# A two-layer decoder trunk: RMSNorm factors sent through DRAM instead of TensorE, and their sums over four column groups

## The chip, the cores and the metric

The kernel runs on one core of a Trainium2 chip. The metric is the device time of one execution, in microseconds (us). A core has five engines that run side by side, each through its own list of instructions in order: TensorE (PE in the profile, with its weight loads as PEld), VectorE (DVE), ScalarE (ACT), GpSimd (POOL) and SyncE (SP). All matrix products end in PSUM, a small memory in eight banks; everything else lives in SBUF, a memory of 128 partitions, or in DRAM, which DMA transfers reach.

## The reference

Two layers; in each, one RMSNorm feeds two token mixers, and their gated sum goes through an output projection into the residual stream. There are 512 tokens and 16 learned meta tokens ahead of them (T = 528), a width of 1024 and fp32 data.

```python
h = rmsnorm(h_res, norm_gain[l])                  # over 1024 channels
proj = h @ w_in[l]
u_pool, z_pool, c_q, c_kv, k_rope, z_mla, g_pool, g_mla = jnp.split(proj, IN_SPLIT_POINTS, axis=-1)
y_pool = (pool_mix(u_pool, pool_w_group[l], pool_scale[l]) * jax.nn.silu(z_pool)) @ pool_w_up[l]
o_mla = mla(c_q, c_kv, k_rope, pos, ...)          # 8 heads; c_kv is normed over 256 channels
y_mla = (o_mla * jax.nn.silu(z_mla)) @ mla_w_up[l]
merged = jax.nn.sigmoid(g_pool) * y_pool + jax.nn.sigmoid(g_mla) * y_mla
h_res = h_res + merged @ w_out[l]
```

`pool_mix` takes, for four groups of 128 channels, the mean over the last 2, 4, 8 or 16 tokens minus the token itself, and multiplies by a 128 x 128 matrix. A norm's factor is 1/sqrt(mean of squares + eps), one number per token; two of them matter here, that of h and that of c_kv.

## The kernel before

**Layout.** Channels lie on partitions and tokens along the free dimension, so a tile is 128 channels x 528 tokens. A projection (class `Gemm`) makes one such tile: for each 128 rows of its weights, three matmuls (`mm3`, L190 to L192) on high and low halves of weights and data, which together give nearly fp32 precision. The first layer and the whole-sequence tiles of the second go in two segments of 264 tokens (`FULL`); other tiles of the second layer go in one of 512 (`XS`).

**Factors after the product.** The product is taken on data that isn't normed, and the factor of each token is applied when a tile is evicted from PSUM. So u (L491), the gates (L500, L563, L882) and k_rope (L446) multiply by `inv`, and the k tiles by `cinv` (L574). Both are tiles of 128 equal rows x 528 tokens: a row has to be spread over all partitions.

**How the factors are made** (`norm_sums`). The squares of the eight x tiles (`xsq`) and of the two c_kv tiles (`csq`) are summed over partitions by matmuls with a matrix of ones, 32 columns wide (L363). `tile_position=(0, g)` puts such a matmul on the column group g (0, 32, 64 or 96) of the array. Before, the x sums of the two segments are in groups 0 and 64, and the c sums in 32 and 96. The sums are copied to SBUF (L370), five small transposes (L375, L376) turn them into one number per partition, and VectorE runs three Newton steps for the inverse root on a 128 x 10 tile (`newton`, L294 to L300). For the way back, `rows` transposes the result to rows (L404 to L407), ScalarE copies it to `kinv` (L409, L410), and `spread` multiplies it by a selection matrix, so that each row appears on all 128 partitions (L286), and copies that to SBUF (L287). A similar return exists in the kernel for the keys' factors: eight rows go to DRAM (`kdr`, L692) and come back as broadcasts (`bc`, L701).

**The order of the work.** A generator (`stream`) walks through the projections in the order in which `register` lists them and adds up planned TensorE time: n/2.4 ns for a matmul of n columns. `Layer.go` runs beside it. `up(name)` takes the stream to the end of a projection, `fill_now(ns)` takes it on by so much planned time, and what `go` issues in between stands at that place in program order. Weights come in chunks of 128 x 512, loaded from SP's queue (L114; three buffers) and split into halves by ScalarE (L185) and VectorE (L186); kr's weights are multiplied by the norm gain instead (L181). The framework's planner then lays out each engine's list: program order is the priority, and an instruction whose inputs, by the planner's own times, aren't ready yet is passed by later ones. So the Newton steps on VectorE have splits and evictions between them.

**The stretch in question.** ckv0, ckv1, cq0 to cq2, u0, k0, u1, kr, k1, u2, k2, u3, k3, cq3, v, the four zp with y0 to y2, cq4, y3, cq5. `norm_sums` starts behind ckv1. The first that needs `inv` is the eviction of u0, the first that needs `cinv` that of k0. `tables` (sine and cosine for the rotary part, L304 to L314, layer 0 alone) comes behind u0. `mix(m)` builds the windowed mean of group m by m+1 additions on GpSimd (L513) and two to four VectorE operations (L516 to L520), and splits it for y(m).

Of the kernel before, what the change touches and what calls it, by code (L numbers as in the profile page):

```python
# [18 lines left out]
P = 128  # L19
DEPTH = 2  # L20
D = 1024
SEQ = 512
NM = 16
T = SEQ + NM
HALF = T // 2
W = 528
WU = 544
# [19 lines left out]
C_MM, C_VBD, C_INVF, C_CNT = 356, 372, 380, 381  # L47
# [7 lines left out]
LAG = 2000.0  # L55
BATCH = 8
SPL = 240
WARM = 8


# [11 lines left out]
def trunk(ctx, tc, xT, pos, win, wkr, wqb, wkb, wvb, wgr, wpu, wmu, wout, gains, const, yT):  # L72
    nc = tc.nc
    pe, act, dve, gp, sp = nc.tensor, nc.scalar, nc.vector, nc.gpsimd, nc.sync

    cp = ctx.enter_context(tc.tile_pool(name="cp", bufs=1))
# [22 lines left out]
    def mmt():  # L99
        return pp.tile([P, 512], F32, tag="mm", name=nm("mm"), bufs=4)  # L100
# [4 lines left out]
    FULL = [(0, HALF), (HALF, T)]  # L105
# [30 lines left out]
        pe.matmul(wps[:, 0:P], ones, ones, start=True, stop=True)  # L136
    maskw = cp.tile([P, 512], BF16, name="maskw")
    gp.memset(maskw[:, :512 - P], 0.0)
    kinv = cp.tile([34, T], F32R, name="kinv")
    sel = cp.tile([64, 2], F32R, name="sel")  # L140
    gp.memset(sel.bitcast(F32), 0.0)
    for i in range(2):
        gp.memset(sel[32 * i:32 * i + 2, i:i + 1].bitcast(F32), 1.0)
    identr = cp.tile([P, P], F32R, name="identr")

    def other_loads(made):
# [28 lines left out]
    def wload(src, n, gain, spare):  # L175
        raw = early.pop(0) if early else fetch(src, n, rawt(), sp)
        loads[0] += 1
        pool, th, tl, nb = (tp, "th", "tl", 2) if loads[0] <= 2 or spare else (wp, "whi", "wlo", 3)
        if gain is not None:
            v = raw[:, :n].rearrange("p (k m) -> p k m", k=8)  # L180
            dve.tensor_mul(v, v, gain.unsqueeze(2).to_broadcast([P, 8, n // 8]))  # L181
            return raw, None
        hi = pool.tile([P, W if pool is tp else 512], F32R, tag=th, name=nm("whi"), bufs=nb)
        lo = pool.tile([P, W if pool is tp else 512], F32R, tag=tl, name=nm("wlo"), bufs=nb)
        act.activation(hi[:, :n], raw[:, :n], AF.Copy)  # L185
        dve.tensor_sub(lo[:, :n], raw[:, :n], hi[:, :n].bitcast(F32))  # L186
        return hi, lo

    def mm3(out, wh, wl, xh, xl, start, stop):
        pe.matmul(out, wh, xh, start=start, stop=False)  # L190
        pe.matmul(out, wh, xl, start=False, stop=False)  # L191
        pe.matmul(out, wl, xh, start=False, stop=stop)  # L192

    plan = []
    done = set()

# [77 lines left out]
    def fill_now(ns):  # L274
        end = clk[0] + ns
        while clk[0] < end and step():
            pass
# [2 lines left out]
        act.activation(hi[:, a:b], src, AF.Copy)  # L280
        dve.tensor_sub(lo[:, a:b], src, hi[:, a:b].bitcast(F32))  # L281

    def spread(dst, i):
        for a, b in FULL:
            ps = mmt()[:, :b - a]
            pe.matmul(ps, sel[0:34, i:i + 1].to_broadcast([34, P]), kinv[:, a:b], start=True, stop=True)  # L286
            act.activation(dst[:, a:b], ps, AF.Copy)  # L287

    def behind(ins, other):
        tc.add_manual_dep(ins.ins, other.ins.name,  # L290
                          mybir.DependencyInfo(mybir.DependencyClass.Sync, mybir.DependencyReason.DATA))
# [22 lines left out]
        dve.tensor_scalar(tcos, tcos, -2.0, 1.0, op0=ALU.mult, op1=ALU.add)  # L314

    scr = dp.tile([P, 8, SEQ], F32, name="scr")
    kdr = [dp.tile([H, T], F32, name=f"kdr{l}") for l in range(DEPTH)]

    hbuf = [(slot(f"hh{k}", F32R), slot(f"hl{k}", F32R)) for k in range(8)]

    class Layer:
# [32 lines left out]

        def norm_sums(self):
            fill_now(2600)
            ps = [mmt(), mmt()]
            for t, r, start, stop in [(self.xsq[k], 0, k == 0, k == 7) for k in range(6)] + [
                    (self.csq[0], 32, True, False), (self.xsq[6], 0, False, False),
                    (self.xsq[7], 0, False, True), (self.csq[1], 32, False, True)]:  # L360
                for s, (a, b) in enumerate(FULL):
                    r_ = r + 64 * s
                    mm = pe.matmul(ps[s][r_:r_ + 32, :HALF], ones[:, 0:32], t[:, a:b], start=start, stop=stop,  # L363
                                   tile_position=(0, r_))
                    if t is not self.csq[1]:
                        behind(mm, self.csq_last)
            sums = tmp()
            rep = sm.tile([64, 8, NM], F32, tag="rep", name=nm("rep"))
            for s, (a, b) in enumerate(FULL):
                act.activation(sums[0:64, a:b], ps[s][64 * s:64 * s + 64, :HALF], AF.Copy)  # L370
            dve.tensor_copy(rep, sums[0:64, 0:NM].unsqueeze(1).to_broadcast([64, 8, NM]))
            fill_now(2600)
            ps = mmt()[:, 0:165].rearrange("p (j c) -> p j c", c=33)
            for j in range(4):
                pe.transpose(ps[:, j, :], sums[0:33, NM + P * j:NM + P * (j + 1)], ident[0:33, 0:33])  # L375
            pe.transpose(ps[:, 4, :], rep[0:33].rearrange("p a b -> p (a b)"), ident[0:33, 0:33])  # L376
# [4 lines left out]
            dve.tensor_scalar(na[:, 0, :], ps[:, :, 0], 1.0 / D, EPS, op0=ALU.mult, op1=ALU.add)  # L381
            dve.tensor_scalar(self.eps, na[:, 0, :], EPS, None, op0=ALU.mult)
            dve.scalar_tensor_tensor(out=na[:, 1, :], in0=ps[:, :, 32], scalar=1.0 / 256, in1=self.eps,
                                     op0=ALU.mult, op1=ALU.add)
            newton(ny, na, nt)
            w = tmp()
            gp.memset(w[:, 0:170], 0.0)
            v = w[:, 0:170].rearrange("p (j c) -> p j c", c=34)
            nv = ny.rearrange("p a j -> p j a")
            nh = sm.tile([P, 5, 2], F32R, tag="nh", name=nm("nh"))  # L390
            dve.tensor_copy(nh, nv)
            dve.tensor_copy(v[:, :, 0:33:32], nh.bitcast(F32))
            dve.tensor_sub(v[:, :, 1:34:32], nv, nh.bitcast(F32))
            fill_now(8200)
            self.rows(v, 34, kinv)
            self.inv, self.cinv = slot("rinv"), slot("cq9")
            fill_now(1300)
            spread(self.inv, 0)
            spread(self.cinv, 1)
            self.st = [sct(), sct()]  # L400

        def rows(self, v, n, out):
# [103 lines left out]
        def mix(self, m):  # L506
            u, x0 = self.us[m], self.x0
            s = u
            for e in range(m + 1):
                w = 1 << e  # L510
                lo_ = 2 * w if not self.last else NM + 2 * w - 1
                n = tmp(WU)
                gp.tensor_tensor(out=n[:, lo_:WU], in0=s[:, lo_:WU], in1=s[:, lo_ - w:WU - w], op=ALU.add)  # L513
                s = n
            f = tmp()
            dve.scalar_tensor_tensor(out=f[:, x0:T], in0=s[:, NM + x0:WU], scalar=1.0 / (2 << m),  # L516
                                     in1=u[:, NM + x0:WU], op0=ALU.mult, op1=ALU.subtract)
            if not self.last:
                dve.tensor_mul(f[:, 0:NM], s[:, NM:2 * NM], cst[:, C_CNT + NM * m:C_CNT + NM * (m + 1)])
# [398 lines left out]
        def register(self, nxt):  # L918
# [11 lines left out]
            def cq(m):  # L930
                add(f"cq{m}", wi(MT_CQ + m), D, evac=self.ev_cq(m), xs=hs, segs=XS)
# [1 line left out]
            def kk(p):  # L933
                add(f"k{p}", wkb[l, p], 256, evac=self.ev_k(p), xs=cs, segs=FULL)

            for m in range(3):
                cq(m)
            for m in range(4):
                add(f"u{m}", wi(MT_U + m), D, evac=self.ev_u(m), xs=hs, segs=FULL)
# [6 lines left out]
            def y(m):  # L946
                add(f"y{m}", wgr[l, m], P, evac=self.ev_y(m), xs=lambda: [self.ys[m]], segs=XS)

            cq(3)
            add("v", wvb[l], 1024, body=self.v_body)  # L950
            zp(0)
            zp(1)
# [2 lines left out]
            y(1)  # L955
            zp(3)
            y(2)
            cq(4)
            y(3)
            cq(5)  # L960
            for r in range(2):
                add(f"qr{r}", wqb[l, r], 768, evac=self.ev_qr(r), xs=lambda: self.cqs, segs=XS)
            for p in range(4):
# [20 lines left out]
        def go(self, nxt):  # L984
# [11 lines left out]
                for k in range(8):  # L996
                    self.square_x(k)
            self.norm_sums()
            up("u0")
            if l == 0:  # L1000
                tables()
            up("u1")
            self.mix(0)
            self.mix(1)
            up("u3")
            self.mix(2)
            up("cq3")
            self.mix(3)
            up("qr1")
            for s, (a, b) in enumerate(FULL):  # L1010
                a0 = max(a, self.x0)
# [108 lines left out]
```

## Time and profile before

| | |
|---|---|
| median of 3 runs | 800.36 us (799.65 to 800.38) |
| the profiled execution's own time | 799.36 us |
| its span, first to last instruction | 797.6 us |
| TensorE clock granted | 1.00 |
| TensorE, VectorE, ScalarE, GpSimd busy | 790.3, 528.1, 416.0, 194.4 us |
| DMA | 80.71 MB, mean 101 GB/s |

The profile is of one execution. Its page gives busy times by engine, the chain of work that ended last, and groups of instructions by line; the timeline lists instructions with start and duration in us, and in brackets the idle time ahead of one with what ended it. Matmul durations overlap, since one starts while the last still drains, so starts are what to compare.

### The profile page before, as it was taken

What the parts mean: (1) busy time and instruction counts of PE and PEld (TensorE: products, weight loads), DVE (VectorE), ACT (ScalarE), POOL (GpSimd) and SP (SyncE); (2) the same over time, 40 slices, a digit from 0 to 9 for tenths busy, and PEclk for the clock granted to TensorE, in tenths of its full rate; (3) what the DMA queues carried; (4) which work ended last, traced back from release to release, by engine and by line L of the source; (5) the groups of instructions that cost most, each with busy time, mean ns of one, the idle gap of its engine ahead of it and who ended that gap; (6) DMA issues with size and microseconds to landing.
All of it is one profiled execution on the core that took longest, in us unless ns stands there. A gap on an engine that the chain in (4) does not pass through costs nothing.

```text
span 797.6 us, 14595 instructions
## 1 busy us (share of the span) xinstructions
PE 790.3 (99%) x5329; PEld 711.8 (89%) x5329; DVE 528.1 (66%) x1136; ACT 416.0 (52%) x943; POOL 194.4 (24%) x262
## 2 busy tenths in 40 slices
PE   9999999999999999999999999999999999999998
PEld 8889999999999999999997997877788888887887
DVE  5568767437689987685354686665467889665942
ACT  8455645644556665543354456446455666654421
POOL 1024404003333322142000163021024333410600
PEclk9999999999999999999999999999999999999999
DMA  6222233335233222324642222334252322222373
GB/s 241 74 70 91 72 100 90 110 86 146 79 88 89 79 67 67 89 87 145 179 142 73 73 88 87 94 84 119 81 165 89 101 83 78 71 70 77 93 225 105
DMA packets 48872, 80.71 MB, mean 101 GB/s; under 512 B 5904, under 2 KB 14480, under 8 KB 48800
## 3 DMA queue, kind: packets, MB, share of 16 engines
q1 hardware_dynamic: 48656, 79.52, 33.2%
q8 instruction: 42, 0.69, 0.4%
q10 hardware_dynamic: 144, 0.26, 0.1%
q14 instruction: 30, 0.25, 0.1%
HBM read 73.40 MB, written 4.23 MB: 97 GB/s over the span
## 4 chain that ended last, share of the span: by engine, by line
PE 96%; DMA 2%; ACT 1%; DVE 1%; issue 0%; POOL 0%; ACTq 0%; POOLq 0%
PE mm L190 28%; PE mm L192 27%; PE mm L191 27%; PE mm L805 2%; PE S L191 2%; PE S L192 2%; PE S L190 1%; PE o L811 1%; PE o L810 1%; PE mm L363 1%; PE S L472 1%; DMA xb<-xT 1%; DMA bc<-kdr 1%; PE mm L430 0%; DMA rinv<-win 0%; DMA raw<-wmu 0%
## 5 line engine op out<-in xcount | busy, mean ns | idle before, releaser
L190 PE MATMUL mm<-hh,whi 128*128 128x264 f32 (+2 forms) x1096 | 346.0, 318 | 0.5 <-ACT whi L185 0.3
L191 PE MATMUL mm<-hl,whi 128*128 128x264 f32 (+2 forms) x1096 | 343.4, 314 | 0.0
L192 PE MATMUL mm<-hh,wlo 128*128 128x264 f32 (+2 forms) x1096 | 342.1, 315 | 0.0
L186 DVE TENSOR_TENSOR wlo<-raw,whi 128x512 fp32r<-128x512 f32 (+2 forms) x251 | 186.5, 746 | 115.0 <-ACT whi L185 108.2
L185 ACT ACTIVATE whi<-raw 128x512 fp32r<-128x512 f32 (+2 forms) x251 | 150.2, 601 | 182.6 <-PE mm L191 136.9
L190 PEld LDWEIGHTS mm<-hh,whi 128*128 128x128 f32 x1096 | 205.6, 188 | 13.8 <-ACT racc L819 0.5
L191 PEld LDWEIGHTS mm<-hl,whi 128*128 128x128 f32 x1096 | 206.2, 188 | 12.2 <-issue 0.4
L192 PEld LDWEIGHTS mm<-hh,wlo 128*128 128x128 f32 x1096 | 205.0, 188 | 12.7 <-issue 0.4
L711 POOL TENSOR_TENSOR tmp<-kp,bc 64x528 f32<-64x528 f32 x16 | 24.5, 1530 | 115.0 <-DMA bc<-kdr 79.8
L550 POOL TENSOR_TENSOR racc<-racc,tmp 128x264 f32<-128x264 f32 (+1 forms) x15 | 14.1, 941 | 142.8 <-ACT tmp L549 142.7
L783 POOL TENSOR_TENSOR pm<-pa,rs 128x16 f32<-128x16 f32 x32 | 11.6, 363 | 143.9 <-DVE rs L778 143.9
L893 POOL TENSOR_TENSOR tmp<-tmp,xb 128x264 f32<-128x264 f32 (+1 forms) x24 | 27.1, 1152 | 58.1 <-DVE tmp L891 33.0
L739 DVE CUSTOM_DVE_ANT_0 S<-S,maskw,nqs 128x272 f32<-128x272 f32 (+4 forms) x80 | 38.4, 498 | 1.6 <-PE S L192 1.2
L746 ACT ACTIVATE cq<-S,bia 128x400 f32<-128x400 f32 (+2 forms) x48 | 24.6, 517 | 22.0 <-DVE bia L773 12.2
L190 PE MATMUL mm<-u,whi 128*128 128x264 f32 (+1 forms) x108 | 35.2, 326 | 0.0
L192 PE MATMUL mm<-cq,wlo 128*128 128x264 f32 (+1 forms) x108 | 34.8, 323 | 0.0
L192 PE MATMUL mm<-u,wlo 128*128 128x264 f32 (+1 forms) x108 | 34.8, 322 | 0.0
L191 PE MATMUL mm<-cq,whi 128*128 128x264 f32 (+1 forms) x108 | 34.7, 322 | 0.0
L190 PE MATMUL mm<-cq,whi 128*128 128x264 f32 (+1 forms) x108 | 34.7, 322 | 0.0
L281 DVE TENSOR_TENSOR tl<-mm,th 128x512 fp32r<-128x512 f32 (+1 forms) x64 | 29.3, 481 | 6.8 <-ACT th L280 5.8
L785 POOL TENSOR_TENSOR cq<-cq,rs 128x384 f32<-128x384 f32 (+1 forms) x32 | 32.4, 1012 | 0.0
L280 ACT ACTIVATE th<-mm 128x512 fp32r<-128x512 f32 (+1 forms) x64 | 25.5, 433 | 10.3 <-PE mm L805 10.0
(266 smaller groups left out, 1374.4 us busy)
## 6 DMA issues: line engine op xcount, KB each, us to landing
raw<-win SPq DMA_DIRECT2D x143, 256.0 KB, 2.6
raw<-wout SPq DMA_DIRECT2D x32, 256.0 KB, 3.1
bc<-kdr SPq DMA_DIRECT2D x16, 264.0 KB, 3.7
raw<-wpu SPq DMA_DIRECT2D x16, 256.0 KB, 2.7
raw<-wmu SPq DMA_DIRECT2D x16, 256.0 KB, 2.6
raw<-wqb SPq DMA_DIRECT2D x12, 256.0 KB, 2.7
tmp<-xT SPq DMA_DIRECT2D x16, 132.0 KB, 3.3
tmp<-scr SPq DMA_DIRECT2D x7, 256.0 KB, 3.5
```

The lines of the kernel that those rows point to most:

```text
L185: act.activation(hi[:, :n], raw[:, :n], AF.Copy)
L186: dve.tensor_sub(lo[:, :n], raw[:, :n], hi[:, :n].bitcast(F32))
L190: pe.matmul(out, wh, xh, start=start, stop=False)
L191: pe.matmul(out, wh, xl, start=False, stop=False)
L192: pe.matmul(out, wl, xh, start=False, stop=stop)
L280: act.activation(hi[:, a:b], src, AF.Copy)
L281: dve.tensor_sub(lo[:, a:b], src, hi[:, a:b].bitcast(F32))
L711: gp.tensor_mul(kf[r0:r0 + 64, :], self.kp[r0:r0 + 64, :], bc[r0:r0 + 64, :])
L739: dve.tensor_tensor_reduce(out=sv, in0=sv, in1=mask, scale=nqs[:, i, h:h + 1], scalar=3e38, op0=ALU.add, op1=ALU.min, accum_out=bia[:, c:c ...
L746: act.activation(pv, sv, AF.Exp, scale=-1.0, bias=bia[:, i:i + 1], accum_out=rs[:, c:c + 1])
L785: gp.tensor_mul(pt[i][:, NM:], pt[i][:, NM:], rs[:, i:i + 1].to_broadcast([P, n - NM]))
L893: gp.tensor_add(t[:, :b - a], t[:, :b - a], self.am[m][:, a:b])
```

## The change

1. The sums use all four column groups for both kinds: of each pair of tiles the even one goes to group 64s, the odd one to 64s + 32, for segment s. The x sums have one PSUM bank, the c sums another. Two numbers per token and kind are left and are added on VectorE after the transposes, which are now 97 columns wide instead of 33. VectorE copies the c sums, ScalarE the x sums, and the transposes wait for ScalarE's last copy.
2. `kinv`, `sel`, `spread` and the norm's call of `rows` go. The Newton result is written element by element from 128 partitions to two rows in DRAM (`ndr`), and each row is read back as a broadcast to 128 partitions. The broadcasts are issued after `fill_now(RET)`, 12500 planned ns, and depend on the newest matmul issued by then (`behind`).
3. cq3 and cq4 move ahead of u0; cq5 takes cq4's old place.
4. `tables` moves from behind u0 to between the writes and the broadcasts. Layer 0's fill ahead of the transposes is 3900 instead of 2600.
5. `mix` is parted: `window` (GpSimd) and `mix` (VectorE, ScalarE). Group 2's `mix` comes behind zp0 instead of u3, group 3's behind zp1 instead of cq3.
6. kr's weights are multiplied on GpSimd instead of VectorE.

```diff
-            dve.tensor_mul(v, v, gain.unsqueeze(2).to_broadcast([P, 8, n // 8]))
+            gp.tensor_mul(v, v, gain.unsqueeze(2).to_broadcast([P, 8, n // 8]))
...
+    ndr = [[dp.tile([1, T], F32, name=f"ndr{l}{i}") for i in range(2)] for l in range(DEPTH)]
...
-            ps = [mmt(), mmt()]
-            for t, r, start, stop in [(self.xsq[k], 0, k == 0, k == 7) for k in range(6)] + [
-                    (self.csq[0], 32, True, False), (self.xsq[6], 0, False, False),
-                    (self.xsq[7], 0, False, True), (self.csq[1], 32, False, True)]:
+            px, pc = mmt(), mmt()
+            runs = [(px, self.xsq[k], k, k < 2, k >= 6) for k in range(8)] + [(pc, self.csq[m], m, True, True) for m in range(2)]
+            for k in range(0, 10, 2):
                 for s, (a, b) in enumerate(FULL):
...
+                    for ps, t, m, start, stop in runs[k:k + 2]:
+                        g = 64 * s + 32 * (m % 2)
+                        mm = pe.matmul(ps[g:g + 32, :HALF], ones[:, 0:32], t[:, a:b], start=start, stop=stop,
+                                       tile_position=(0, g))
...
-                act.activation(sums[0:64, a:b], ps[s][64 * s:64 * s + 64, :HALF], AF.Copy)
...
+                copied = act.activation(sums[0:64, a:b], px[64 * s:64 * s + 64, :HALF], AF.Copy)
+                dve.tensor_copy(sums[64:128, a:b], pc[64 * s:64 * s + 64, :HALF])
...
-            fill_now(2600)
+            fill_now(2600 if self.l else 3900)
...
-                pe.transpose(ps[:, j, :], sums[0:33, NM + P * j:NM + P * (j + 1)], ident[0:33, 0:33])
+                behind(pe.transpose(ps[:, j, :], sums[0:97, NM + P * j:NM + P * (j + 1)], ident[0:97, 0:97]), copied)
...
-            fill_now(8200)
-            self.rows(v, 34, kinv)
-            self.inv, self.cinv = slot("rinv"), slot("cq9")
-            fill_now(1300)
-            spread(self.inv, 0)
-            spread(self.cinv, 1)
+            self.inv, self.cinv = slot("rinv"), slot("q1")
+            for i, d in enumerate((self.inv, self.cinv)):
+                row = ndr[self.l][i]
+                sp.dma_start(row[0, NM:T].rearrange("(j p) -> p j", p=P), ny[:, i, 0:4])
+                sp.dma_start(row[0, 0:NM].rearrange("(p j) -> p j", j=1), ny[0:NM, i, 4:5])
+            if self.l == 0:
+                tables()
+            fill_now(RET)
+            for i, d in enumerate((self.inv, self.cinv)):
+                behind(sp.dma_start(d[:, 0:T], ndr[self.l][i].partition_broadcast(P)), newest[0])
...
-            for m in range(3):
+            for m in range(5):
                 cq(m)
...
-            cq(3)
...
-            cq(4)
+            cq(5)
             y(3)
-            cq(5)
...
-            up("u0")
-            if l == 0:
-                tables()
             up("u1")
-            self.mix(0)
-            self.mix(1)
+            for m in range(2):
+                self.mix(m, self.window(m))
             up("u3")
-            self.mix(2)
-            up("cq3")
-            self.mix(3)
+            s2 = self.window(2)
+            up("k3")
+            s3 = self.window(3)
+            up("zp0")
+            self.mix(2, s2)
+            up("zp1")
+            self.mix(3, s3)
```

More of the change, by code (lines that the diff above doesn't have):

```diff
@@ L57 @@
 SPL = 240
+RET = 12500.0
 WARM = 8
@@ L138, in trunk @@
     gp.memset(maskw[:, :512 - P], 0.0)
[L139 to L143, printed above, removed]
     identr = cp.tile([P, P], F32R, name="identr")
@@ L191, in mm3 @@
         pe.matmul(out, wh, xl, start=False, stop=False)
-        pe.matmul(out, wl, xh, start=False, stop=stop)
+        newest[0] = pe.matmul(out, wl, xh, start=False, stop=stop)
+    newest = [None]
     plan = []
@@ L281, in split @@
         dve.tensor_sub(lo[:, a:b], src, hi[:, a:b].bitcast(F32))
[L283 to L287, printed above, removed]
     def behind(ins, other):
@@ L361, in norm_sums @@
                 for s, (a, b) in enumerate(FULL):
[L362 to L366, printed above, removed]
+                    for ps, t, m, start, stop in runs[k:k + 2]:
+                        g = 64 * s + 32 * (m % 2)
+                        mm = pe.matmul(ps[g:g + 32, :HALF], ones[:, 0:32], t[:, a:b], start=start, stop=stop,
+                                       tile_position=(0, g))
+                        if t is not self.csq[1]:
+                            behind(mm, self.csq_last)
@@ L367, in norm_sums @@
             sums = tmp()
-            rep = sm.tile([64, 8, NM], F32, tag="rep", name=nm("rep"))
+            rep = sm.tile([P, 8, NM], F32, tag="rep", name=nm("rep"))
             for s, (a, b) in enumerate(FULL):
-                act.activation(sums[0:64, a:b], ps[s][64 * s:64 * s + 64, :HALF], AF.Copy)
-            dve.tensor_copy(rep, sums[0:64, 0:NM].unsqueeze(1).to_broadcast([64, 8, NM]))
-            fill_now(2600)
-            ps = mmt()[:, 0:165].rearrange("p (j c) -> p j c", c=33)
+                copied = act.activation(sums[0:64, a:b], px[64 * s:64 * s + 64, :HALF], AF.Copy)
+                dve.tensor_copy(sums[64:128, a:b], pc[64 * s:64 * s + 64, :HALF])
@@ L374, in norm_sums @@
+            dve.tensor_copy(rep, sums[:, 0:NM].unsqueeze(1).to_broadcast([P, 8, NM]))
+            fill_now(2600 if self.l else 3900)
+            ps = mmt()[:, 0:485].rearrange("p (j c) -> p j c", c=97)
             for j in range(4):
-                pe.transpose(ps[:, j, :], sums[0:33, NM + P * j:NM + P * (j + 1)], ident[0:33, 0:33])
-            pe.transpose(ps[:, 4, :], rep[0:33].rearrange("p a b -> p (a b)"), ident[0:33, 0:33])
+                behind(pe.transpose(ps[:, j, :], sums[0:97, NM + P * j:NM + P * (j + 1)], ident[0:97, 0:97]), copied)
@@ L377, in norm_sums @@
+            pe.transpose(ps[:, 4, :], rep[0:97].rearrange("p a b -> p (a b)"), ident[0:97, 0:97])
             na = sm.tile([P, 2, 5], F32, tag="na2", name=nm("na2"))
@@ L381, in norm_sums @@
             dve.tensor_scalar(na[:, 0, :], ps[:, :, 0], 1.0 / D, EPS, op0=ALU.mult, op1=ALU.add)
+            dve.scalar_tensor_tensor(out=na[:, 0, :], in0=ps[:, :, 32], scalar=1.0 / D, in1=na[:, 0, :],
+                                     op0=ALU.mult, op1=ALU.add)
             dve.tensor_scalar(self.eps, na[:, 0, :], EPS, None, op0=ALU.mult)
-            dve.scalar_tensor_tensor(out=na[:, 1, :], in0=ps[:, :, 32], scalar=1.0 / 256, in1=self.eps,
-                                     op0=ALU.mult, op1=ALU.add)
+            for c in (64, 96):
+                dve.scalar_tensor_tensor(out=na[:, 1, :], in0=ps[:, :, c], scalar=1.0 / 256,
+                                         in1=self.eps if c == 64 else na[:, 1, :], op0=ALU.mult, op1=ALU.add)
             newton(ny, na, nt)
[L386 to L393, printed above, removed]
-            fill_now(8200)
-            self.rows(v, 34, kinv)
-            self.inv, self.cinv = slot("rinv"), slot("cq9")
-            fill_now(1300)
-            spread(self.inv, 0)
-            spread(self.cinv, 1)
+            self.inv, self.cinv = slot("rinv"), slot("q1")
[8 more added lines that the diff above has]
+                behind(sp.dma_start(d[:, 0:T], ndr[self.l][i].partition_broadcast(P)), newest[0])
             self.st = [sct(), sct()]
@@ L504, in ev_silu, with window, mix @@
             return ev
-        def mix(self, m):
-            u, x0 = self.us[m], self.x0
-            s = u
+        def window(self, m):
+            s = self.us[m]
             for e in range(m + 1):
                 w = 1 << e
-                lo_ = 2 * w if not self.last else NM + 2 * w - 1
-                n = tmp(WU)
-                gp.tensor_tensor(out=n[:, lo_:WU], in0=s[:, lo_:WU], in1=s[:, lo_ - w:WU - w], op=ALU.add)
+                if e < m:
+                    a, n, v = 2 * w if not self.last else NM + 2 * w - 1, tmp(WU), 0
+                else:
+                    a, n, v = NM + self.x0, slot(f"q{m}") if m > 1 else tmp(), NM
+                gp.tensor_tensor(out=n[:, a - v:WU - v], in0=s[:, a:WU], in1=s[:, a - w:WU - w], op=ALU.add)
                 s = n
+            return s
+        def mix(self, m, s):
+            u, x0 = self.us[m], self.x0
             f = tmp()
-            dve.scalar_tensor_tensor(out=f[:, x0:T], in0=s[:, NM + x0:WU], scalar=1.0 / (2 << m),
+            dve.scalar_tensor_tensor(out=f[:, x0:T], in0=s[:, x0:T], scalar=1.0 / (2 << m),
                                      in1=u[:, NM + x0:WU], op0=ALU.mult, op1=ALU.subtract)
             if not self.last:
-                dve.tensor_mul(f[:, 0:NM], s[:, NM:2 * NM], cst[:, C_CNT + NM * m:C_CNT + NM * (m + 1)])
+                dve.tensor_mul(f[:, 0:NM], s[:, 0:NM], cst[:, C_CNT + NM * m:C_CNT + NM * (m + 1)])
                 dve.tensor_sub(f[:, 0:NM], f[:, 0:NM], u[:, NM:2 * NM])
```

## The prediction, made before the change was run

> **What bounds the kernel now.** I read the page's busy shares first, then its chain of work that ended last, then TensorE's own timeline around the lines that the diff touches, because that is where the bound can move.
>
> ```profile
> PE 790.3 (99%) x5329; PEld 711.8 (89%) x5329; DVE 528.1 (66%) x1136; ACT 416.0 (52%) x943; POOL 194.4 (24%) x262
> PE 96%; DMA 2%; ACT 1%; DVE 1%; issue 0%; POOL 0%; ACTq 0%; POOLq 0%
> ```
>
> TensorE is hardly ever without an instruction, and the chain is TensorE for 96% of the span. So an edit is worth what it takes out of TensorE's sequence of instructions or puts in; work on other engines is worth nothing until TensorE waits for it. I price each block of small matmuls by the delay that it puts between the large ones. A 264-column matmul of L190 to L192 follows the last after 0.122 us, a 512-column one after 0.232 us. The cost of a block is the time from the last large matmul before it to the second one behind it (the first is slowed too), less as many such steps as lie between.
>
> **The old return path, removed.** In layer 0 it looks like this (start, duration, engine, line):
>
> ```profile
> 39.84 0.28 PE L192 MATMUL mm<-hh,wlo 128*128 128x264 f32 x1
> 40.05 0.19 PE L404 MATMUL mm<-cst,tmp 16*34 16x16 f32 x1
> ...
> 40.53 0.37 PE L190 MATMUL mm<-hh,whi 128*128 128x264 f32 x1
> 40.74 0.28 PE L191 MATMUL mm<-hl,whi 128*128 128x264 f32 x1
> ...
> 41.59 0.28 PE L192 MATMUL mm<-hh,wlo 128*128 128x264 f32 x1
> 41.80 0.63 PE L286 MATMUL mm<-kinv,sel 34*128 34x264 f32 x3
> 42.91 0.39 PE L286 MATMUL mm<-kinv,sel 34*128 34x264 f32 x1 [0.48 <-ACT rinv L287]
> 43.23 0.39 PE L190 MATMUL mm<-hh,whi 128*128 128x264 f32 x1
> 43.46 0.28 PE L191 MATMUL mm<-hl,whi 128*128 128x264 f32 x1
> 43.58 0.28 PE L192 MATMUL mm<-hh,wlo 128*128 128x264 f32 x1
> ```
>
> The transposes of `rows` cost 40.74 - 39.84 - 2 x 0.122 = 0.66 us. The four broadcast matmuls of `spread` cost 43.58 - 41.59 - 3 x 0.122 = 1.62 us, 0.48 of it a wait for ScalarE. In layer 1 the same timeline has `rows` between 444.57 and 445.47 (0.66) and `spread` in two pieces, 448.16 to 449.04 and 449.65 to 450.52 (0.63 each). Sum removed: 0.66 + 1.62 + 0.66 + 1.26 = **4.2 us**. With them go six ScalarE copies a layer (kinv and rinv/cq9, 2.4 us), off the path.
>
> **The sums over four column groups.** Old order, layer 0:
>
> ```profile
> 24.07 0.28 PE L192 MATMUL mm<-hh,wlo 128*128 128x264 f32 x1
> ...
> 28.54 0.25 PE L375 MATMUL mm<-cst,tmp 33*128 33x33 f32 x1 [0.50 <-ACT tmp L370]
> 28.71 0.39 PE L190 MATMUL mm<-hh,whi 128*128 128x264 f32 x1
> 28.94 0.28 PE L191 MATMUL mm<-hl,whi 128*128 128x264 f32 x1
> ```
>
> That is 28.94 - 24.07 - 0.24 = 4.63 us with the wait before the first transpose; the other four transposes come at 31.2 (31.00 to 31.80: 0.56 us). Layer 1: 426.77 to 431.35 less 3 x 0.232 = 3.88, and all five transposes 435.52 to 436.61, 0.63. The records of L363 start in pairs, 0.2225 us apart: two groups run side by side, and groups 0 and 64 carry eight sums of two records each, 16 x 0.2225 = 3.56 us, which leaves 0.32 us for getting in and out. The new order names groups 0, 32, 64, 96 in turn, and each carries four x sums and one c sum, 10 records: 2.23 + 0.32 = 2.55 us if four run side by side. The nearest row says they do. The statistics of L472 name four groups in the same turn:
>
> ```profile
> 71.76 0.28 PE L190 MATMUL mm<-hh,whi 128*128 128x264 f32 x1
> 71.97 1.09 PE L472 MATMUL S<-sq,cst 128*16 128x264 f32 x16
> 73.00 0.39 PE L191 MATMUL mm<-hl,whi 128*128 128x264 f32 x1
> 73.22 0.40 PE L192 MATMUL mm<-hh,wlo 128*128 128x264 f32 x2
> ```
>
> Sixteen records of the same length cost 73.22 - 71.76 - 0.24 = 1.22 us = 4 x 0.2225 + 0.33. The five transposes grow from 33 to 97 columns. Rows: 33 columns step by 0.065 us, 128 columns (L406) by 0.109. Between them, 0.095, so the block is 0.63 + 5 x 0.03 = 0.78 (bounds 0.63 and 0.85). New: 2.55 + 0.78 = 3.33 a layer. Layer 0 saves 4.63 + 0.56 - 3.33 = 1.86, since the manual dependence on the ScalarE copy and the longer fill (3900) give the early transpose no reason to wait; layer 1 saves 3.88 + 0.63 - 3.33 = 1.18. Together **3.0 us**.
>
> **What comes in its place: DMAs.** A layer gets four writes (two of 512 elements of 4 bytes, two of 16) and two broadcasts of 264 KB, all on SP's queue, issued in 0.33 us each. TensorE pays only if the factors come late. In layer 0 the sums now end near 26.8, and the transposes follow after 3900 planned ns, at about 31.1 (planned 264-column steps are 0.110, the trace's 0.122, so a fill takes 1.11 times its figure). Newton took 4.8 us in layer 0 and 5.8 in layer 1 (436.38 to 442.17):
>
> ```profile
> 31.69 0.17 DVE L381 TENSOR_SCALAR na<-mm 128x5 f32<-128x5 f32 x1 [2.95 <-PE mm L376]
> ...
> 36.28 0.17 DVE L300 SCALAR_TENSOR_TENSOR ny<-nt,ny 128x10 f32<-128x10 f32 x1
> ```
>
> With VectorE's other work between its steps, and now perhaps some of the tables, the writes go out near 38. The broadcasts wait for the newest matmul, 12500 x 1.11 = 13.9 us behind the transposes, so at 45; the writes have 7 us to land. A broadcast like them:
>
> ```profile
> bc<-kdr SPq DMA_DIRECT2D x16, 264.0 KB, 3.7
> ```
>
> At most 5.4 us over the 16 of them. So rinv lands near 50. Who needs it first is u0's first eviction. It ran at 48.23 (L491); two cq tiles of 48 x 0.122 = 5.86 us now stand ahead and 4.1 us are gone, hence 55.8. That leaves about 5 us. Layer 1: broadcasts 13.7 us behind the transposes, landed by 19; the eviction lies 23 to 25 behind them. **Cost taken: nothing.**
>
> The element writes are unlike any row. From below: the 4-byte packets of the trace (semaphore updates) take 9 ns at the median, and kdr's write landed in 1.5 us. From above: the smallest data packets, gains' 192 bytes, take 15 ns and at worst 398. Each of 16 engines gets 64 elements for both writes: 0.6 us at 9 ns, 25 us at 398. I take the low end plus a landing, about 3 us, since 128 of those packets, the nearest row, have a median of 15.
>
> The Trainium skill's DMA: Bandwidth & Descriptors, Rules for kernel authors, speaks against such a write: a last dimension that isn't contiguous becomes one descriptor per element, and should be rearranged. Its Bandwidth section has some 10.5 ns a packet and its anatomy a fixed 2.0 us; my estimate from that page is 0.7 + 2.0 = 2.7 us, so the sum stays. No transfer of before shows it.
>
> **SP's queue** is in order, so weight loads planned behind a write or a broadcast wait with it. The load of k0's weights was issued at 33.79 and split at 41.79; it lands in 2.0, so 6 us are spare. A write that holds SP all through Newton would hold it up to 5.8. Hidden, barely, and if not, a part of a microsecond or two.
>
> **The rest.** The tables (some 5.6 us of VectorE, 2.6 of ScalarE with its table load) move from beside u0 and k0 into the cq stage, where VectorE was busy 9.7 of 20 us (24 to 44) against 23.4 of 28 (44 to 72). The multiply of kr's weights (0.43 us on VectorE, once 0.8 of waiting in its queue) becomes one on GpSimd, 0.75 or more; kr is needed ten microseconds later. Two evictions of 64 x 264 fall to VectorE, 0.42 each, beside the fill. mix(2) and mix(3) go behind zp0 and zp1: y2 then still has zp1, zp2 and zp3 ahead, over 15 us of TensorE, against 1.8 us of VectorE each. All nothing; without their cover, a microsecond each.
>
> **Sum.** 4.2 + 3.0 = 7.2 us off the profiled execution's 799.36 (span 797.6 and 1.76 around it): 792.2. The median of the runs shown is 1.0 above that execution, so I forecast 793.2.
>
> **Rivals.**
> - *Sums stay in pairs.* Then 40 records a layer are 20 pairs, 20 x 0.2225 = 4.45 us, 2.2 more than reckoned: 4.4 us back in two layers, 797.6. Against it stands L472's block. 0.07.
> - *New waits eat half.* Evictions and splits in the denser u and k stage, or factors 2 us late in both layers: 4 back, 797. For it: VectorE is at 84% there already, and the planned order shifts everywhere. 0.16.
> - *Slower: SP is held by the element writes.* The broadcasts wait for their landing, u0's eviction stands at the head of VectorE's queue, and splits behind it starve TensorE. Break-even: 7 us until the broadcast, 5 until the eviction, 1.5 of k0's matmuls, 3.6 to use up half of the gain's 7.2: writes of 17 us, 0.27 us an element. At 0.398 us they last 25: 8 us more a layer, 800.4 + 16 = 816. For it: a packet did take that long, and nobody here has written elements. Against: the median. 0.12.
> - *It doesn't do what it says* (blocks stay on TensorE): no, the diff drops the calls.
>
> Beside the third stands a rule of the Trainium skill, TensorE: Matmul & The Clock Gate, HAM oscillation: gaps over about 3.4 us halve TensorE's clock. By it each such wait would cost some 1.7 us more, an estimate from that page, 820 in all. The trace grants 1.00 throughout and has no wait over 1.1 us, so no run here shows it.
>
> **Chances.** Forecast 0.62 (791.4 to 795), pairs 0.07, half 0.16, slower 0.12, near nothing 0.03. Two runs of this kernel can't be told apart within 0.2% (1.6 us); part of the half case falls there: faster 0.80, same 0.07, slower 0.13. Range 791.0 to 798.5, from small transposes with a further wait gone to the half case.
>
> **What would show it.** Right: no L286 or first `rows` on TensorE, L363's block near 2.5 us, u0's eviction waiting for TensorE and not for a DMA. Wrong: TensorE waiting for a split or an eviction after 50 us, a write landing after more than 7 us, or L363 starting in pairs.

## The result and the profile after

The changed kernel takes 793.35 us (median of 6 runs, 792.05 to 794.51) against 800.17 (6 runs): ratio 0.9915, 95% interval 0.9902 to 0.9928, or 6.8 us less. The forecast was 793.2. Its profiled execution has a span of 791.4 us, 6.2 less than before. (Ratios and intervals are those on record; a ratio can differ from the quotient of the two medians by about 0.001, and "us less" goes by the ratio unless the text says otherwise.)

```profile
PE 784.4 (99%) x5311; PEld 709.4 (90%) x5311; DVE 528.5 (67%) x1136; ACT 410.6 (52%) x931; POOL 195.9 (25%) x259
PE 96%; DMA 2%; DVE 1%; ACT 1%; issue 0%; POOL 0%; DVEq 0%; ACTq 0%; POOLq 0%
```

TensorE is as full as before; it has fewer instructions. (L186 to L188 are now the large matmuls, L355 the sums, L368 and L369 the transposes, L483 u's eviction, L385 and L386 the writes, L391 the broadcasts.) The sums in layer 0, on TensorE's timeline:

```profile
24.54 0.28 PE L188 MATMUL mm<-hh,wlo 128*128 128x264 f32 x1
24.75 1.10 PE L355 MATMUL mm<-cq,ones 128*32 128x264 f32 x16
25.66 1.52 PE L355 MATMUL mm<-q,ones 128*32 128x264 f32 x24
27.11 0.39 PE L186 MATMUL mm<-hh,whi 128*128 128x264 f32 x1
27.34 0.28 PE L187 MATMUL mm<-hl,whi 128*128 128x264 f32 x1
```

The block costs 27.34 - 24.54 - 0.24 = 2.56 us, where 2.55 was reckoned: forty records in ten turns of four. The transposes come later, one, three and one, with no wait ahead of them. Between the large matmuls of 30.02 and 31.51 lie eight steps, so they cost 31.51 - 30.02 - 8 x 0.122 = 0.51 us in all, and 0.48 in layer 1. Nothing of L286 or of the first `rows` is left.

What came in their place is on SP's queue (start, time to issue, line):

```profile
41.90 0.50 SPq L386 DMA_DIRECT2D ndr<-ny  x1
42.50 0.37 SPq L115 DMA_DIRECT2D raw<-win  x1
48.16 0.33 SPq L391 DMA_DIRECT2D rinv<-ndr  x1
50.76 0.32 SPq L391 DMA_DIRECT2D q<-ndr  x1
51.17 0.38 SPq L115 DMA_DIRECT2D raw<-wkb  x1
```

The view of the DMA issues (KB each, median us to landing):

```profile
ndr<-ny SPq DMA_DIRECT2D x4, 2.0 KB, 8.0
ndr<-ny SPq DMA_DIRECT2D x4, 0.1 KB, 8.2
```

A write of 2 KB takes 8 us to land. In layer 0 the second write lands at 48.1 and the fourth at 50.7, and each broadcast is issued right then. So it is the landing, not the newest matmul, that releases the broadcasts, and SP stands still from 42.9 to 48.2 with weight loads behind it. TensorE notices once:

```profile
58.34 0.28 PE L188 MATMUL mm<-kh,wlo 128*128 128x264 f32 x1
59.03 0.36 PE L186 MATMUL mm<-hh,whi 128*128 128x264 f32 x1 [0.40 <-DVE u L483]
```

The factors are not what is late there. u0 is done on TensorE at about 57.2, and the broadcast of cinv, the later of the two, landed at 54.3. But VectorE's list has the split of a chunk of weights ahead of u0's eviction, and weights are late:

```profile
52.40 0.63 ACT L181 ACTIVATE whi<-raw 128x512 fp32r<-128x512 f32 x1 [4.54 <-DMA raw<-win]
57.64 0.90 DVE L182 TENSOR_TENSOR wlo<-raw,whi 128x512 fp32r<-128x512 f32 x1 [1.04 <-ACT whi L181]
58.46 0.76 DVE L483 TENSOR_TENSOR u<-mm,rinv 128x264 f32<-128x264 f32 x2
```

Some loads are late because SP issues them behind the broadcasts (from 51.2 on). But the load that SP issued at 42.5, before it stood still and right behind the writes, was not split before 52.4 either; in layer 1 the load in the same place took 10.2 us to land, where the one ahead of layer 0's writes took 2.4. The element writes hold up what is issued behind them, in flight as well as on SP.

**The account between the two spans.** Return path gone: -4.2 us (all four of its blocks). Sums with transposes: 9.70 before (4.63 + 0.56 + 3.88 + 0.63), 6.11 after (2.56 + 0.51 in layer 0, 2.56 + 0.48 in layer 1): -3.6. The wait at u0: +0.4. The matmuls of the first ten microseconds go at the pace of the loads of x, and one of these came 0.5 later (the row that stood at 9.95 is at 10.41): +0.5. The wait for the first head's keys (S from kh) is 0.9 instead of 0.4: +0.5. Sum -6.4, against -6.2 between the spans; the 0.2 left are smaller differences in both directions that were not followed up. The last two terms lie outside the edits.

### The profile page after: what moved, and what is told of

It reads as the page before. It is cut to its first block, busy times and chain, and to the rows that moved or that the text cites. A ratio compares the mean times of both kernels' runs of the same rounds, so it can differ in the third digit from the quotient of the medians.

```text
span 791.4 us, 14564 instructions
## 1 busy us (share of the span) xinstructions
PE 784.4 (99%) x5311; PEld 709.4 (90%) x5311; DVE 528.5 (67%) x1136; ACT 410.6 (52%) x931; POOL 195.9 (25%) x259
## 4 chain that ended last, share of the span: by engine, by line
PE 96%; DMA 2%; DVE 1%; ACT 1%; issue 0%; POOL 0%; DVEq 0%; ACTq 0%; POOLq 0%
PE mm L186 28%; PE mm L188 28%; PE mm L187 28%; PE mm L802 2%; PE S L187 2%; PE S L188 1%; PE S L186 1%; PE o L808 1%; PE o L807 1%; PE S L464 1%; DMA xb<-xT 1%; DMA bc<-kdr 1%; PE mm L355 1%; PE mm L422 0%; DMA rinv<-win 0%
## 5 line engine op out<-in xcount | busy, mean ns | idle before, releaser
L186 PE MATMUL mm<-hh,whi 128*128 128x264 f32 (+2 forms) x1096 | 346.4, 318 | 0.6 <-DVE u L483 0.4
L188 PE MATMUL mm<-hh,wlo 128*128 128x264 f32 (+2 forms) x1096 | 342.8, 315 | 0.0
L186 PEld LDWEIGHTS mm<-hh,whi 128*128 128x128 f32 x1096 | 205.8, 188 | 14.3 <-issue 1.0
L188 PEld LDWEIGHTS mm<-hh,wlo 128*128 128x128 f32 x1096 | 205.3, 188 | 12.9 <-issue 0.9
L780 POOL TENSOR_TENSOR pm<-pa,rs 128x16 f32<-128x16 f32 x32 | 11.3, 353 | 145.2 <-DVE rs L775 145.2
L186 PE MATMUL mm<-u,whi 128*128 128x264 f32 (+1 forms) x108 | 35.2, 326 | 0.0
L188 PE MATMUL mm<-u,wlo 128*128 128x264 f32 (+1 forms) x108 | 34.8, 322 | 0.0
L186 PE MATMUL mm<-cq,whi 128*128 128x264 f32 (+1 forms) x108 | 34.8, 322 | 0.0
L188 PE MATMUL mm<-cq,wlo 128*128 128x264 f32 (+1 forms) x108 | 34.6, 322 | 0.0
L187 PE MATMUL mm<-kn,whi 128*128 128x264 f32 (+1 forms) x96 | 30.6, 320 | 0.0
```

What stands on the lines that cost most here:

```text
L188: newest[0] = pe.matmul(out, wl, xh, start=False, stop=stop)
```

## The experiments

The theory was that time goes where TensorE's sequence gets shorter, and that all else is hidden. The rivals were waits for the factors, a held SP queue, and side edits that are worth more than nothing.

**The sums alone.** The kernel before with the new `norm_sums` up to Newton; the old return and order stay.

> The kernel before with the new sums alone (four column groups, 97-column transposes, layer 0's fill of 3900); factors still return by transposes, kinv and spread, and the order of the projections is the old one. Theory (the gain is what leaves TensorE's sequence, block by block): the prediction's terms give 3.0 us less than before, and the blocks as the changed kernel's trace has them give 3.4 (layer 0: 4.63 + 0.56 less 2.56 + 0.60; layer 1: 3.88 + 0.63 less 2.56 + 0.57), so a ratio of 0.9957 to 0.9963. Rival (the gain comes from the order of the projections, the tables and the mixing stages, or from the return alone): ratio 1.000. Theory: L355's block of 2.5 to 2.6 us in each layer; rival: pairs or a wait of TensorE that eats the difference.

796.12 against 799.52, ratio 0.9951 (0.9937 to 0.9964), 3.9 us less (3.4 by the medians) where 3.4 was expected; with the transposes at 0.51 and 0.48 the blocks give 3.6. The block of the sums is 2.56 us in layer 0 again. The sums pay by themselves, whatever the order of the projections.

**The return alone.** The changed kernel with the old `norm_sums` up to Newton.

> The changed kernel with the old sums (two pairs of groups, 33-column transposes, fill 2600); the return through DRAM, the order, the tables and the mixing stages are those of the change. Theory: the return's share alone, 4.2 us less than before, less 0.4 for the wait at 58.5 us that the changed kernel shows: 795.9 to 796.4 where before is 800.2, ratio 0.9948 to 0.9955. Rival (the parts aren't additive, because the sums' end sets when the DMAs start and SP is held): with sums that end 1.3 us later the broadcasts come later too, TensorE waits longer at u0 in both layers, and the ratio is 0.997 or more.

796.46, ratio 0.9956 (0.9943 to 0.9969), 3.5 us less, its range just short of the expected one. TensorE waits 0.4 us at u0 as in the change, and 0.5 ahead of the early transpose as before. The two parts add up: 0.9951 x 0.9956 = 0.9907, against 0.9915 together.

**No tiles to hide behind.**

```diff
-RET = 12500.0
+RET = 9500.0
-            for m in range(5):
+            for m in range(3):
                 cq(m)
...
+            cq(3)
             add("v", wvb[l], 1024, body=self.v_body)
...
-            cq(5)
+            cq(4)
             y(3)
+            cq(5)
```

> The changed kernel with cq3, cq4 and cq5 in their old places, so that two gate tiles less stand between the writes and u0; the broadcasts come after 9500 planned ns instead of 12500 (the old fills' sum), since at 12500 they would stand behind their reader. Theory: the return is hidden only by these two tiles. In the changed kernel's trace rinv is issued at 48.2 and lands by 51.1, and u0's eviction would now come 11.7 us earlier than 58.5 less its wait, at about 46 in layer 0 and 45 in layer 1 with rinv landing at 450.6 for an eviction due at 444.5; four PSUM buffers give TensorE 1.5 us more. So 3 to 5 us of waiting in each layer: 800 to 804, and TensorE waiting for VectorE's L483. Rival (the DMAs are hidden anyway, the order costs nothing): 793.4 plus or minus 1.

810.01 against 799.52, ratio 1.012 (1.0103 to 1.0138): slower than the kernel before, and by more than expected. The waits of TensorE, and layer 0, where u0's eviction waits for rinv itself:

```profile
PE mm L186 <- DVE u L483: 11.3, 2, 6.0
```

```profile
52.31 0.77 DVE L483 TENSOR_TENSOR u<-mm,rinv 128x264 f32<-128x264 f32 x2 [8.35 <-DMA rinv<-ndr]
52.89 0.56 PE L186 MATMUL mm<-hh,whi 128*128 128x264 f32 x1 [6.04 <-DVE u L483]
```

Behind such a wait the matmuls are slow too. By stretches (busy us of PE, PEld, DVE, ACT, POOL; then PEclk, DMA share, GB/s):

```profile
53.00:57.00 4.00, 4.00 (x20) 4.00 (x20) 3.16 (x9) 2.64 (x6) 1.90 (x2) 0.53 0.44 113
57.00:62.00 5.00, 5.00 (x58) 4.30 (x60) 2.95 (x5) 1.26 (x2) 0.69 (x1) 1.00 0.16 54
459.00:463.00 4.00, 4.00 (x20) 4.00 (x20) 2.94 (x6) 2.37 (x6) 1.37 (x1) 0.51 0.48 138
```

The granted clock is 0.53 and 0.51 for 4 us behind each wait, which costs 4 x 0.47 + 4 x 0.49 = 3.8 us. With the waits of 11.3 that is 15.1, of which the change has 0.4 too. The profiled run has 808.0, and the change's ratio puts this chip's level at 0.9915 x 799.5 = 792.7: 15.3 more. The wait is the prediction's slower rival, with the cover taken away instead of the writes made longer. That gaps of TensorE halve its clock is what the Trainium skill's TensorE: Matmul & The Clock Gate, HAM oscillation, has; here the trace shows it.

**The order alone.** The kernel before with cq3 and cq4 ahead of u0, `tables()` ahead of the old return, the later mixing stages and kr's multiply on GpSimd.

> The kernel before with the order of the change alone: cq3 and cq4 ahead of u0, the tables ahead of the old return, mix parted and its stages 2 and 3 a gate tile later, kr's weights multiplied on GpSimd; sums and return are the old ones (cinv in the slot q1). Theory: nothing leaves TensorE's sequence, so ratio 1.000, within 0.001, the spread's wait of 0.48 us in layer 0 perhaps gone. Rival (the order itself pays, by less crowding of VectorE beside u and k): 2 us or more less, ratio under 0.9975.

804.35, ratio 1.005 (1.0032 to 1.0068): 4.0 us slower (4.8 by the medians), so neither theory nor rival. The tables run ahead of the old return's small VectorE steps, and the transposes of `rows` wait for them:

```profile
40.95 0.28 PE L193 MATMUL mm<-hh,wlo 128*128 128x264 f32 x1
43.00 0.17 PE L409 MATMUL mm<-cst,tmp 16*34 16x16 f32 x1 [1.77 <-DVE tmp L396]
```

In that run `rows` and `spread` cost 4.56 us in layer 0 and 2.6 in layer 1, against 2.3 and 1.9 before, and the clock is 0.50 from 45 to 50 us, some 2.5 more. That is 5.5 us, where the profiled spans differ by 4.4, so something else in this order may have gained a microsecond; it was not followed up. In this combination the order doesn't pay. What it would pay with the tables behind the old return was not tried.

**When the broadcasts are planned.** `RET = 6000.0`, then `RET = 16000.0`, nothing else.

> The changed kernel with the broadcasts planned 6000 ns behind the writes instead of 12500. In the changed kernel's trace SP issues the last write at 41.9 us and one weight load at 42.5, then nothing until rinv's broadcast at 48.2, when the first write has landed, and the next weight load comes at 51.2. With 6000 the broadcast of rinv stands ahead of the load of 42.5 too. Theory (a DMA that waits on SP for the writes' landing holds the weight loads behind it, and they have some 6 us to spare): that load comes 6 us later, at 48.5, and TensorE waits up to 2 us more in each layer, ratio 0.992 to 0.997. Rival (the hold costs nothing at all, SP is held by the landing either way): ratio as the change's, 0.990 to 0.9925.

794.82 against 800.1, ratio 0.9940 (0.9926 to 0.9954): within the theory's range, and its interval ends just above the rival's; it overlaps the change's own (0.9902 to 0.9928) by a hair. TensorE has new waits for splits, 0.6 us on ScalarE's and 0.4 on VectorE's, most of it in layer 1. The load that the change issued at 42.5 goes out at 48.78, behind rinv's broadcast, but it is split at 53.1, only 0.7 later than in the change, where it was held up behind the writes. So in layer 0 holding it on SP costs little.

> The changed kernel with the broadcasts planned 16000 ns behind the writes instead of 12500, so that two weight loads a layer go ahead of them and SP hardly waits for the landing. Theory (the wait of 0.4 us at 58.5 in layer 0 comes from weight loads held by the broadcasts; the factors have time left): that wait goes, ratio 0.9905 to 0.992, the same as the change within the spread. Rival (the broadcasts themselves are what is late): rinv lands some 2 us later in both layers, TensorE waits for L483, ratio 0.994 or more.

793.2, ratio 0.9919 (0.9906 to 0.9932): no difference from the change. The wait didn't go, it moved: TensorE waits for L483 0.3 us in layer 0 and 0.8 in layer 1, where rinv is issued at 453.4, some 6 us later than in the change, and VectorE waits 1.0 for it. By these traces 12500 stands between held loads and late factors; the totals show a difference for 6000 at most.

**Does the order of issue matter?** Same groups, same PSUM banks, other order.

```diff
-            for k in range(0, 10, 2):
-                for s, (a, b) in enumerate(FULL):
-                    for ps, t, m, start, stop in runs[k:k + 2]:
+            for part in (0, 1):
+                for k in range(part, 10, 2):
+                    for s, (a, b) in enumerate(FULL):
+                        ps, t, m, start, stop = runs[k]
```

> The changed kernel with the same sums in the same column groups, issued in another order: first the even tiles (groups 0 and 64), then the odd ones (32 and 96). Theory (groups run side by side only if neighbours in the order of issue): pairs, 20 x 0.2225 + 0.3 = 4.8 us a block instead of 2.56, so 4.4 us more than the change, ratio 0.9965 to 0.9975. Rival (TensorE picks free groups itself out of its queue): the blocks stay at 2.6 us and the ratio at 0.990 to 0.9925.

794.56, ratio 0.9932 (0.9918 to 0.9946), and the block:

```profile
24.13 0.28 PE L188 MATMUL mm<-hh,wlo 128*128 128x264 f32 x1
...
28.28 0.28 PE L187 MATMUL mm<-hl,whi 128*128 128x264 f32 x1
```

28.28 - 24.13 - 0.24 = 3.91 us, between the theory's 4.8 and the rival's 2.6. So the order matters: for most of the block four groups have work and only two run. But it is 16 turns and not 20: around the seam, from 25.7 to 26.6, both pairs run. Why TensorE mixes there was not settled. The two blocks come to 2.7 us more than in the change. The profiled spans differ by just that, the ratios by 1.4, with intervals that overlap and admit both.

**What a write by elements costs.** Extra writes that nothing reads, in layer 0.

> The changed kernel with five extra writes to DRAM in layer 0 that nothing reads, far apart in time: 128 elements of 4 bytes, 512 as in the change, 1280, the same 1280 as 128 runs of 40 bytes, and 16 elements. In the changed kernel the writes of 512 and of 16 elements behind them took 8 us from issue to landing, where I had reckoned with 3. Theory A (the landing goes by the number of elements, some 0.1 us for each of an engine's share of them): 128 lands in 3 to 4 us, 512 in 7 to 8, 1280 in 14 to 18, the 128 runs and the 16 elements in 2 to 4. Theory B (a fixed price for a write with small pieces): all five land in 7 to 8 us.

This one told little of the sizes, since all five writes went out close together, from 43.6 to 62.7 us. It did show the price of many (821.32 in the one run). TensorE stood 19 us at u0, and again for weights and not for the factors: rinv landed at 62.1, 12 us after its issue, but a load that SP issued at 63.2, behind the writes, was not split before 83.9, and u0's eviction comes after that split.

```profile
83.94 1.30 ACT L181 ACTIVATE whi<-raw 128x512 fp32r<-128x512 f32 x2 [18.89 <-DMA raw<-win]
84.60 0.69 DVE L182 TENSOR_TENSOR wlo<-raw,whi 128x512 fp32r<-128x512 f32 x1 [20.03 <-ACT whi L181]
85.21 0.77 DVE L484 TENSOR_TENSOR u<-mm,rinv 128x264 f32<-128x264 f32 x2
```

> The five extra writes to DRAM of the last probe once more (128, 512 and 1280 elements of 4 bytes, 1280 as 128 runs of 40 bytes, 16 elements; nothing reads them), now each tied to the newest matmul and spread from y0 to pu6 in layer 0, since without that tie they all went out at 44 to 63 us, one behind the other. Theory A (the landing goes by the number of pieces): about 3 us for 128 elements, 7 to 8 for 512, 14 to 18 for 1280, 2 to 4 for the runs and for 16. Theory B (a fixed price): 7 to 8 us for each. With either, weight loads issued behind the long one land late, and the time is some microseconds above the change's.

Now they stand apart. By write, issue line and landing:

```profile
L1003 SPq DMA_DIRECT2D prb<-ny x1: 1100/1100/1100, 148.7 to 148.7; - x1
...
DMA to landing us min/median/max: 13.0/13.0/13.0
```

```profile
L1003 SPq DMA_DIRECT2D prb<-ny x1: 326/326/326, 168.6 to 168.6; - x1
...
DMA to landing us min/median/max: 2.2/2.2/2.2
```

The first is 1280 elements: 13.0 us. The second is the same 5 KB as 128 runs of 40 bytes: 2.2 us. Sixteen elements alone land in 1.3. The trace gives no landing for the probes of 128 and 512. That is theory A: the price goes with the number of pieces and not with the bytes. It is 13.0 us for 80 elements on each of 16 engines, if they are spread evenly: 0.16 us each. It fits the change, where 1056 elements (66 an engine) take from 40.5 to 50.7 us, and where 16 elements behind 512 land late. Whether the count alone does it is not shown: in the first probe neighbouring elements also come from different partitions, in the second each partition writes a run of its own. (823.02 in one run; its waits were not taken apart.)

**The side edits undone.** `tables` behind u0, `mix(2)` at u3, `mix(3)` at k3, kr's multiply on VectorE.

> The changed kernel with three of its side edits undone: the tables behind u0, mix(2) at u3 and mix(3) at k3 (cq3's old neighbour), kr's multiply on VectorE. Theory (these edits cost and bring nothing, since other engines have room): ratio as the change's, 0.990 to 0.993. Rival (they keep VectorE free beside u and k, where it was 84% busy before): TensorE waits for evictions or splits between 58 and 90 us and in v, 1 us or more in all, ratio 0.9935 or more.

798.68 against 799.55, ratio 0.9988 (0.9979 to 0.9997). The theory fell: without these edits 5 to 6 us of the 6.8 are lost. Its trace has TensorE waiting for splits and evictions, 2.6 us of it for v's:

```profile
PE mm L186 <- DVE vt L593: 2.6, 1, 2.6
PE mm L186 <- DVE u L481: 1.1, 2, 0.6
```

and the clock is 0.51 from 95 to 100 us, which alone costs some 2.4 us. I took the mixing stages for the larger part, and tried them alone:

> The changed kernel with the mixing stages alone put back: mix(2) at u3, mix(3) at k3; the tables stay ahead of the broadcasts and kr's multiply on GpSimd. The run that undid all three lost about 5 us to the change, and its trace has waits of TensorE in three places: 1.6 us at 65 to 68 (u's evictions behind the tables' last steps), 3.3 us at 90 to 94 (v's evictions L593 beside mix(2) and mix(3), with TensorE's clock at 0.51 in the 5 us behind), 0.7 us in layer 1. Theory (the mixing stages beside v are the larger part): the wait at v comes back, 3 to 5 us more than the change, ratio 0.995 to 0.998. Rival (the tables are): the wait at v doesn't come back and the ratio is 0.993 or less.

793.28 against 799.39, ratio 0.9928 (0.9914 to 0.9941): by the ratio as the rival says, though a wait of 0.9 us at v is there. The waits at u are not, and the clock stays at 1.00. So the later mixing stages are worth about a microsecond at most while the tables are early. What the full undoing lost hangs on the tables, or on kr's multiply, or on their meeting with the mixing stages; these were not tried apart, and it stays open which.

**Layer 0's fill.** `fill_now(2600)` in both layers.

> The changed kernel with layer 0's fill ahead of the transposes at 2600, as before, instead of 3900. Theory (the dependence on ScalarE's last copy alone keeps the transposes from being planned too early, the longer fill is slack): the transposes of layer 0 cost 0.6 us without a wait, ratio as the change's, 0.990 to 0.993. Rival (the fill is what takes the wait away): TensorE waits 0.4 to 0.6 us for the copies before the transposes as in the kernel before, ratio some 0.0006 more, and that wait is seen in the trace.

793.95, ratio 0.9929 (0.9916 to 0.9941). The rival's wait is in the trace:

```profile
PE mm L368 <- ACT tmp L362: 0.8, 1, 0.8
```

The total can't tell 0.8 us from the spread. The fill, not the dependence, takes the wait away.

## Why the prediction was right, point by point

- **TensorE's sequence is the bound, priced block by block**: right. The removed blocks are gone whole, the new sums came to 2.56 us for 2.55, and each half alone gave its share. That the total came within 0.2 us of the forecast is partly luck: the blocks gave 7.8 us where 7.2 was reckoned, and 1.4 us of waits and late loads that the sum doesn't have (0.4, 0.5 and 0.5) went the other way in the profiled execution.
- **Four groups side by side**: right, and L472's block of before was the right row. The transposes were over-sized: 0.51 and 0.48 us, not 0.78, as wide as they are.
- **The element writes**: the term was mis-sized. I took 3 us from the 4-byte and 192-byte packets (9 and 15 ns); they land 7.2 to 9.1 us after their issue, at 0.16 us an element. My own sign of being wrong, a landing after more than 7 us, came true, and the total held all the same. The packets' times in the trace don't contain this, since the 512 packets of such a write are over within a microsecond and the landing comes some six or more later. The bound held: under the break-even of 0.27. The writes also went out at 40.5 and not near 38. The cover until u0's eviction took all of the factors' delay up. My estimate from the Trainium skill's DMA: Bandwidth & Descriptors, Bandwidth and Anatomy of one DMA, 2.7 us, was too low as well (its figures there are of DMAs issued from GpSimd, and these are issued from SP). The page's advice against single elements, in Rules for kernel authors, was right, and the measured 8 us decides.
- **SP's queue**: right that it is hidden barely; 0.4 us shows at u0, and planning the broadcasts 6.5 us earlier seems to cost a little more. What the step left out is that loads issued behind the writes are late even where SP doesn't hold them: 10 us to land instead of 2.4.
- **"All nothing; without their cover, a microsecond each"**: half right. The side edits cost nothing, but without them the change would have kept about a microsecond of its gain. A reading that was not tested apart: with cq3 gone from between k3 and v, VectorE has no light tile left there, and the tables' steps beside u and k push it behind. The warning was in the numbers (23.4 of 28 us busy) and in the rival of new waits, and not in this step.
- **The clock rule**: right as a rival's surcharge, 1.9 us for each of the two waits where I had estimated 1.7, and shown only in runs where TensorE had to wait.

## What to carry to other kernels

When one engine is full, price an edit by the gaps between that engine's large instructions, block by block, and check that whatever replaces the block has cover until its first reader; the cover is part of the change. A DMA that scatters single elements is cheap in bytes and slow to land: look at issue to landing, not at packet times, and at the loads that are issued behind it. Small matmuls on free column groups overlapped fully here only where neighbours in the order of issue named different groups.

## What the runs showed of the hardware that was not expected

- Writes of 4-byte elements to DRAM: 16 elements 1.3 us, 512 about 8 (two such writes and two of 16 one behind the other), 1280 elements 13.0; the same 1280 as 128 runs 2.2.
- A weight load of 256 KB issued right behind four such writes took 10.2 us to land in layer 1, where one ahead of the writes took 2.4.
- A wait of TensorE of 2.6 us (side edits undone; the matmuls around it start 3.0 us apart) was followed by some 5 us at a granted clock of 0.51. The Trainium skill's TensorE: Matmul & The Clock Gate has some 3.4 us in HAM oscillation; here a shorter gap was enough, and the measurement decides. With the order alone, 4.4 us between two large matmuls, with waits of 1.8 and 0.4 and only small matmuls in them, had the same effect (0.50).
- The order in which matmuls on four column groups are issued changes a block from 2.56 to 3.91 us.
